# A two-layer trunk on one core: the attention's softmax steps in a fixed order of TensorE, and an operand tile 80 bytes further down

## The chip, the cores and the metric

The kernel runs on one core of a Trainium2 chip. The metric is the device time of one execution in microseconds (us). TensorE (PE) multiplies matrices; PEld is its loading of weights, which overlaps the multiplication. VectorE (DVE), ScalarE (ACT) and GpSimd (POOL) work element by element, SyncE (SP) issues the DMAs. Results of TensorE land in eight PSUM banks of 128 x 512 floats; everything else lies in SBUF. The three runs of the kernel before took 1333.64 us in the median (1331.63 to 1338.09).

## The reference

A trunk of two layers on 512 tokens of width 1024. Each layer is a mixer and then a SwiGLU feed-forward net, each inside a norm, a modulation by a conditioning vector (`c` times `ada_w`), and a second norm with a gate. The first mixer is a hybrid of pooling and a recurrence; the second, with which the change deals, is dilated attention:

```python
DIL_GROUPS = ((128, 1), (512, 4), (2048, 16))     # window, dilation
...
s = jnp.einsum('brnqhe,brnkhe->brnhqk', qs, kk) + bias
s = jnp.where(mask[None, None, :, None], s, -jnp.inf)
m = jnp.max(s, axis=-1, keepdims=True)
p = jnp.exp(s - m)
l = jnp.sum(p, axis=-1, keepdims=True)
...
w = l_all * jnp.exp(m_all - jnp.max(m_all, axis=0, keepdims=True))
o = jnp.sum(w * o_all, axis=0) / jnp.sum(w, axis=0)
...
return dilated_attention_mixer(h @ att_w_qkv[j], rel_bias) @ att_w_out[j]
...
def swiglu(h, w_in, w_out):
    a, b = jnp.split(h @ w_in, 2, axis=-1)
    return (jax.nn.silu(a) * b) @ w_out
```

There are 3 groups of 8 heads of 64 columns. The last step weights the groups by their sums, so the eight outputs of 64 columns are each one softmax over the keys of three groups.

## The kernel before, in words

Every large product is made of three matmuls in a rounded format: a value is split into a high part and a rest, and high by high, high by rest and rest by high are added in a PSUM bank. `split_into` splits operands, `split_next` the weights: ScalarE copies the high part (L351), VectorE or GpSimd subtracts (L284). All these matmuls go through the helper `mm` (L263). The moved operands lie in tile `h` (the layer's input, high and rest, 2 x 8 x 512 columns) or in `o`, the weights in `r`, in the "swing" tiles that change their owner between stages, and, while `o` and `h` are not needed for operands, there too.

Tile `o` (L197) is made 48 floats longer than its four units of 512 floats, and the slice that is used starts `O_OFF` floats in. By the program's addresses in a partition, `r`, `h` (behind its own offset) and the swing tiles begin at byte 128 of a block of 256; `o` begins at byte 64, that is 192 bytes past the others. The operands that move out of `o` are those of `out_project` when it is called without `late` (`operand`, `rr.get(n // HT, "o")`), for the first mixer's and for both feed-forward output products.

The attention layer runs in `attention` (from L1220). `project_head` makes the queries and keys of pair 0 of heads. Then `values(g, tiles)` makes, for each group g, the values in four PSUM banks: four blocks of 24 matmuls with 512 columns, in each of which one weight matrix is used up; after each block `ada_step` puts two products for the modulation of later stages (L403, 128 x 1025 elements) into VectorE's program, each with its own DMA. A pair of heads takes four steps r = 0 to 3 (quarter of the queries). In each the scores of both heads of three groups are made (28 short matmuls, L1329), VectorE adds the bias and takes the maximum (L1359), ScalarE takes the exponential and the sum (L1364), VectorE the reciprocal (L1366) and the product with it (L1367), TensorE transposes (L1370, eight of 128 x 128), and ScalarE copies the transposed weights out (L1372). `weighted` multiplies these with the values. Queries and keys of pairs 1 to 3 are six blocks of 24 matmuls a pair (`project`), copied from PSUM by `keep_qk` (L1236 on ScalarE, L1238 on VectorE). The output product with `w_ao` is `out_project` with `late`: 24 matmuls of 256 columns for each of four inputs, the first token half first, around the two halves of the weighted sum of pair 3.

The program is written stage by stage: all values, then pair by pair its queries and keys, its four steps, its weighted sum. A planner turns this order into one instruction list for each engine, by its own estimates of when an operand is there; a list is then executed in its order. `hold(...)` forbids it this for the engines named: they take the order of the program until `release()`. Before, the attention layer's first hold comes in `out_project`, after the third input of `w_ao`; up to there TensorE's order is the planner's, except that the two heads' scores alternate by added dependencies. Biases are loaded by SP (`load_biases`, six DMAs a pair, L1257), into tiles that the planner's order makes free.

Of the kernel before, what the change touches and what calls it, by code (L numbers as in the profile page):

```python
# [13 lines left out]
F32R = mybir.dt.float32r  # L14
# [4 lines left out]
P = 128  # L19
# [16 lines left out]
W0 = 259  # L36
# [7 lines left out]
O_OFF, H_OFF = 48, 8  # L44
# [136 lines left out]
def trunk(ctx: ExitStack, tc: tile.TileContext, a: dict, out: bass.AP, last: int = 3):  # L181
# [15 lines left out]
    rr.add("o", sb.tile([P, O_UNITS * UNIT + O_OFF], F32R, tag="o", name="o")[:, O_OFF:], O_UNITS)  # L197
# [558 lines left out]
    def out_project(s, base, n, srcs, ada_until, late=None):  # L756
# [3 lines left out]

        sets = [late[0], None] if late else [[bk.get() for _ in range(4)] for _ in range(2)]
# [414 lines left out]
    chain = out_project(0, w_ho, 8, mix_r, 20, (out_banks, EARLY, end_of_mixer, none, none))  # L1176
# [43 lines left out]
    def attention(s, chain):  # L1220
# [42 lines left out]
        def values(g, tiles):  # L1263
            vb = {c: bk.get() for c in tiles}
            for kk in range(4):
                hi, lo = weights(w_av + 4 * g + kk)
                for k in (2 * kk, 2 * kk + 1):
                    wh, wl = hi[:, (k % 2) * T : (k % 2 + 1) * T], lo[:, (k % 2) * T : (k % 2 + 1) * T]
                    for c in tiles:
# [10 lines left out]
            for c in tiles:  # L1280
                act.activation(VV[g][:, c, :], bk[vb[c]], AF.Copy)
                bk.free(vb[c])

        for g in range(3):
            values(g, (0, 1, 2, 3))

        o_rs = []
        for pair in range(4):
            qk_rs = []
            pt_rs = [ar.get(4) for _ in range(2)]  # L1290
            for x in (pair, pair + 1):
                if x < 4 and x not in biases_of:
                    load_biases(x)
            bias_r, bias_t = biases_of[pair]
            for i in range(6):
                if pair * 6 + i < N_QK:
                    qk_rs.append(head_rs[i])
                    continue
# [6 lines left out]
                qk_rs.append(r)  # L1305
            if pair == 3:
                ahead.update(load=14, split=4, f=2, r=0)
                out_banks = [bk.get() for _ in range(4)]
                rr.add("h", h_t, 2 * ND)
                rr.used["h"] = [k % ND < 4 for k in range(2 * ND)]  # L1310
                for _ in range(2):
                    split_next(0, pool)
                for i, r in enumerate(o_rs):
                    split_into(h_hi[:, i, :], h_lo[:, i, :], ar.ap(r))
                    ar.free(r)
            q0, k0, q1, k1, q2, k2 = (ar.ap(r) for r in qk_rs)
            PT = [ar.ap(r).rearrange("p (r s q) -> p r s q", r=4, s=4) for r in pt_rs]
            halves_of = [slice(64 * hh, 64 * hh + 64) for hh in range(2)]
            by_place = lambda z: z.rearrange("p (r i) -> p r i", r=4)
            two = lambda z: z.rearrange("p (s n) -> p s n", s=2)  # L1320
            for r in range(4):

                banks2 = [bk.get() for _ in range(2)]
                heads2 = list(enumerate(halves_of))[::-1]
                before = [None]

                def score(o, q, k, **kw):

                    i = pe.matmul(o, q, k, start=True, stop=True, skip_group_check=True, **kw).ins  # L1329
                    if before[0]:  # L1330
                        tc.add_manual_dep(i, before[0], NOSYNC, reason="two heads at a time")
                    before[0] = i.name

                qv = q0.rearrange("p (r j i) -> p r j i", r=4, j=4)
                for j in range(4):
                    js = slice(32 * j, 32 * j + 32)
                    for n in range(2 if j == 0 else 1):
                        for hh, ps in heads2:
                            kw = dict(tile_position=(64 * hh, 32 * j))
                            o = bk[banks2[hh]]  # L1340
                            if j == 0 and n == 0:
                                score(o[js, 0:P], far[ps, :], one_row[ps, :], **kw)
                            elif j == 0:
                                score(o[js, P : 2 * P], qv[ps, r, j, :], k0[ps, 0:P], **kw)
                            else:
                                score(o[js, 0 : 2 * P], qv[ps, r, j, :], k0[ps, (j - 1) * P : (j + 1) * P], **kw)
                for i, (q, k) in enumerate(((q1, k1), (q2, k2))):
                    for hh, ps in heads2:
                        qc, kc = (by_place(z)[ps, r, :] for z in (q, k))
                        o = bk[banks2[hh]][:, (2 + i) * P : (3 + i) * P]  # L1350
                        score(o, qc, kc)
                for hh in range(2):
                    b = banks2[hh]
                    sc_r = tr.get(1)
                    sc = tr.ap(sc_r)
                    base = bias_t[:, hh, 255 + r : 256 + r]
                    bias = bass.AP(base.tensor, base.offset, [list(base.ap[0]), [W0 - r, 2], [-1, 256]])
                    m = col(1)
                    dve.tensor_tensor_reduce(  # L1359
                        out=two(sc), in0=two(bk[b]), in1=bias, scale=-1.0, scalar=3e38, op0=ALU.add, op1=ALU.min, accum_out=m  # L1360
                    )
                    bk.free(b)
                    l = col(1)
                    act.activation(sc, sc, AF.Exp, bias=m, scale=-1.0, accum_out=l)  # L1364
                    rl = col(1)
                    dve.reciprocal(rl, l)  # L1366
                    dve.tensor_scalar(sc, sc, rl, None, ALU.mult)  # L1367
                    b = bk.get()
                    for i, seg in enumerate((1, 0, 2, 3)):
                        pe.transpose(bk[b][:, seg * P : (seg + 1) * P], sc[:, i * P : (i + 1) * P], ident)  # L1370
                    tr.free(sc_r)
                    act.activation(PT[hh][:, r, :, :], bk[b].rearrange("p (s q) -> p s q", s=4), AF.Copy)  # L1372
                    bk.free(b)
            for r in qk_rs:
                ar.free(r)
            ar.free(bias_r)

            def weighted(b, first, end):

                todo = []  # L1380
                for kb in range(4):
                    js = [j for j in (kb, kb + 1) if first <= j < end]
                    if js:
                        todo.append((0, kb, js))
# [162 lines left out]
```

## Time and profile before

| | |
|---|---|
| median of three runs | 1333.64 us (1331.63 to 1338.09) |
| profiled execution, time | 1336.7 us |
| profiled execution, span | 1334.9 us |
| TensorE busy | 1265.7 us, 95% |
| PEld / VectorE / ScalarE / GpSimd busy | 84% / 49% / 34% / 20% |
| granted clock of TensorE, mean | 0.97 |
| DMA | 164.25 MB, 123 GB/s in the mean |

A row of a group of instructions gives its line, the engine, the operation, what it writes and reads, how many there are, the busy time and the mean duration of one, and the engine's idle time just before them. Matmuls overlap: a duration in such a row (281 ns) is longer than the distance between two starts. Rows of the timeline give the start, the length, and in brackets the idle time before it and what ended it. In a row of a stretch the granted clock is a share of full speed.

### The profile page before, as it was taken

The page shows a single profiled execution, that of the slowest core. Times are in us where ns is not written, and L with a number is a line of the kernel's source. Part 1 is how long each engine was busy: PE and PEld are TensorE (multiplying, and loading weights), DVE is VectorE, ACT ScalarE, POOL GpSimd, SP SyncE. Part 2 cuts the span into 40 slices and gives each one's busy share as a digit, 9 for nine tenths or more (in the row PEclk, how much of TensorE's full clock was granted, in tenths as well). Part 3 has the DMA queues.
Part 4 walks back from the last instruction along what each step waited for, and adds up shares of the span by engine and source line. Part 5 has one row for each costly group of instructions (what it writes and reads, how often), then busy time and mean ns, then how long its engine had stood idle before and what let it go on. Part 6 is the DMA issues. An engine that isn't in the chain of part 4 may idle for free.

```text
span 1334.9 us, 20663 instructions
## 1 busy us (share of the span) xinstructions
PE 1265.7 (95%) x8672; PEld 1117.5 (84%) x8672; DVE 654.2 (49%) x965; ACT 455.3 (34%) x743; POOL 270.3 (20%) x141
## 2 busy tenths in 40 slices
PE   8897798999999999999999989987999999999997
PEld 6675588998888889999999768776898888889997
DVE  6997975855444223428576233343855222213415
ACT  4241434642222222317333333344552222222313
POOL 3541531411111111212211002030411111121002
PEclk9997899999999999999999899987999999999999
DMA  7855353225554222322277103150226222222301
GB/s 259 321 170 184 103 175 127 84 91 192 197 197 140 79 80 95 127 80 80 96 262 243 48 15 128 38 199 33 88 87 237 79 82 86 69 93 90 104 1 64
DMA packets 50383, 164.25 MB, mean 123 GB/s; under 512 B 5809, under 2 KB 11081, under 8 KB 50290
## 3 DMA queue, kind: packets, MB, share of 16 engines
q1 hardware_dynamic: 50290, 162.93, 35.9%
q8 instruction: 68, 1.11, 0.3%
q14 instruction: 25, 0.20, 0.0%
HBM read 160.78 MB, written 2.13 MB: 122 GB/s over the span
## 4 chain that ended last, share of the span: by engine, by line
PE 80%; DVE 13%; ACT 3%; issue 2%; DMA 2%; POOL 1%; SPq 0%; DVEq 0%; ACTq 0%; POOLq 0%
PE bank L263 76%; DVE ada_w L403 3%; PE bank L1370 1%; PE bank L1329 1%; DVE swing L937 1%; DVE t L1359 1%; DVE r L284 1%; DVE swing L938 1%; DVE swing L284 1%; DVE t L642 1%; ACT t L1364 0%; DVE h L681 0%; DVE f L646 0%; DVE h L539 0%; DMA f<-w_ho 0%
## 5 line engine op out<-in xcount | busy, mean ns | idle before, releaser
L263 PE MATMUL bank<-h,r 128*128 128x512 f32 (+1 forms) x2104 | 470.1, 365 | 15.7 <-DVE f L927 7.9
L263 PEld LDWEIGHTS bank<-h,r 128*128 128x128 f32 x2104 | 367.0, 193 | 79.6 <-ACT h L522 8.7
L263 PE MATMUL bank<-h,swing 128*128 128x512 f32 (+1 forms) x1664 | 325.0, 343 | 3.5 <-ACT swing L351 2.2
L263 PEld LDWEIGHTS bank<-h,swing 128*128 128x128 f32 x1664 | 268.1, 191 | 39.9 <-ACT swing L351 2.4
L284 POOL TENSOR_TENSOR r<-f,r 128x1024 fp32r<-128x1024 f32 x39 | 98.9, 2537 | 430.4 <-PE bank L263 301.1
L263 PE MATMUL bank<-o,swing 128*128 128x256 f32 x1280 | 159.2, 281 | 0.0
L263 PEld LDWEIGHTS bank<-o,swing 128*128 128x128 f32 x1280 | 154.2, 189 | 0.1
L351 ACT ACTIVATE r<-f 128x1024 fp32r<-128x1024 f32 x104 | 109.0, 1057 | 132.1 <-PE bank L263 93.3
L403 DVE SCALAR_TENSOR_TENSOR ada_w<-ada_w,sil 128x1025 f32<-128x1025 f32 x96 | 146.3, 1538 | 15.2 <-DMA ada_w<-ada 14.9
L284 DVE TENSOR_TENSOR r<-f,r 128x1024 fp32r<-128x1024 f32 (+1 forms) x51 | 73.8, 1448 | 161.3 <-PE bank L263 64.0
L284 DVE TENSOR_TENSOR swing<-f,swing 128x1024 fp32r<-128x1024 f32 x45 | 60.0, 1337 | 121.2 <-PE bank L263 81.6
L284 POOL TENSOR_TENSOR swing<-f,swing 128x1024 fp32r<-128x1024 f32 x27 | 66.3, 2456 | 259.3 <-PE bank L263 219.2
L351 ACT ACTIVATE swing<-f 128x1024 fp32r<-128x1024 f32 x80 | 83.5, 1057 | 85.7 <-PE bank L263 42.2
L263 PE MATMUL bank<-o,r 128*128 128x256 f32 x832 | 105.4, 281 | 0.0
L263 PEld LDWEIGHTS bank<-o,r 128*128 128x128 f32 x832 | 101.3, 189 | 0.1
L1193 ACT ACTIVATE t<-bank 128x512 f32<-128x512 f32 (+1 forms) x52 | 27.2, 531 | 175.3 <-PE bank L263 175.3
L263 PE MATMUL bank<-h,o 128*128 128x512 f32 (+1 forms) x312 | 81.6, 347 | 2.5 <-DVE h L681 1.7
L263 PE MATMUL bank<-r,h 128*128 128x512 f32 x288 | 70.9, 395 | 0.0
L263 PEld LDWEIGHTS bank<-r,h 128*128 128x128 f32 x288 | 61.8, 249 | 6.1 <-issue 0.4
L475 POOL TENSOR_TENSOR cst<-cst 128x2 f32<-128x2 f32 (+1 forms) x19 | 17.8, 937 | 232.7 <-DVE cst L473 232.7
L263 PEld LDWEIGHTS bank<-h,o 128*128 128x128 f32 x312 | 56.0, 192 | 10.6 <-DVE h L681 2.1
L284 DVE TENSOR_TENSOR o<-f,o 128x256 fp32r<-128x256 f32 (+2 forms) x37 | 24.5, 678 | 77.3 <-ACT o L565 74.2
(181 smaller groups left out, 1074.4 us busy)
## 6 DMA issues: line engine op xcount, KB each, us to landing
ada_w<-ada SPq DMA_DIRECT2D x96, 512.5 KB, 5.1
f<-w_fi SPq DMA_DIRECT2D x88, 512.0 KB, 4.6
f<-w_fo SPq DMA_DIRECT2D x44, 512.0 KB, 3.4
f<-w_aqk SPq DMA_DIRECT2D x24, 512.0 KB, 3.8
f<-w_av SPq DMA_DIRECT2D x12, 512.0 KB, 6.0
f<-w_qf SPq DMA_DIRECT2D x8, 512.0 KB, 5.2
f<-w_ho SPq DMA_DIRECT2D x8, 512.0 KB, 4.0
f<-x SPq DMA_DIRECT2D x8, 256.0 KB, 3.5
```

The costliest lines, as they stand in the source:

```text
L263: i = pe.matmul(o, lhsT, rhs, start=start, stop=stop, skip_group_check=True)
L284: eng.tensor_tensor(o, x, y, ALU.subtract)
L351: act.activation(hi, w, AF.Copy)
L403: dve.scalar_tensor_tensor(w, w, 1.0, sil, ALU.mult, ALU.mult, accum_out=mods[:, s, 2 * j + k : 2 * j + k + 1])
L475: pool.tensor_tensor(r, v, mhalf[:, 0:cols], ALU.pow)
L642: dve.tensor_tensor(us[i], us[i], rows, ALU.mult)
L937: dve.tensor_tensor(qv, qv, t_first.unsqueeze(2).broadcast_to([P, n, L]), ALU.mult)
L938: dve.tensor_tensor(kv, kv, t_second.unsqueeze(2).broadcast_to([P, n, L]), ALU.mult)
L1193: act.activation(tr.ap(sa)[:, cols], a, AF.Silu)
L1329: i = pe.matmul(o, q, k, start=True, stop=True, skip_group_check=True, **kw).ins
L1359: dve.tensor_tensor_reduce(out=two(sc), in0=two(bk[b]), in1=bias, scale=-1.0, scalar=3e38, op0=ALU.add, op1=ALU.min, accum_out=m)
L1370: pe.transpose(bk[b][:, seg * P : (seg + 1) * P], sc[:, i * P : (i + 1) * P], ident)
```

## The change

Two things change.

**Order.** `values` becomes a generator that stops after each block of 24 matmuls, so does the new `queries_and_keys`, and `fillers` chains 3 x 4 blocks of values and 3 x 6 blocks of queries and keys; `fill_in(n)` runs the next n of them. The softmax step is cut into `scores` and `transposed`. From the first block on TensorE is held to the program's order, which is now written out: scores of steps 0 and 1, a block, transposes of step 0, scores of step 2, a block, and so on. In pair 3 no blocks are left, and its steps stand between the inputs of `w_ao` (`between`, a new sixth entry of `late`, called after each 24 matmuls). TensorE is released before the four engines are held as before. The biases of pair 0 are loaded ahead of the first block, those of pair p + 1 after the last scores of pair p. The tiles `PT` of the transposed weights are allocated once and laid out with the group ahead of the step; heads go 0, 1 instead of 1, 0; the added dependencies go.

**Place.** `O_OFF` goes from 48 to 28 floats. The tile keeps its size, so that nothing else moves; the slice begins 80 bytes lower, at byte 240 of a block of 256, that is 112 bytes past `r` and the swing tiles.

```diff
-O_OFF, H_OFF = 48, 8
+O_OFF, H_OFF = 28, 8
...
-    rr.add("o", sb.tile([P, O_UNITS * UNIT + O_OFF], F32R, tag="o", name="o")[:, O_OFF:], O_UNITS)
+    rr.add("o", sb.tile([P, O_UNITS * UNIT + 48], F32R, tag="o", name="o")[:, O_OFF : O_OFF + O_UNITS * UNIT], O_UNITS)
...
             work = rest(0)
-            for _ in range(late[1] * 3 * ND):
-                next(work)
+            for i in range(late[1]):
+                for _ in range(3 * ND):
+                    next(work)
+                late[5](i)
             late[2]()
             hold(pe, act, dve, pool)
...
+        def queries_and_keys(pair):
             for i in range(6):
...
                 b = bk.get()
                 project(w_qk2 + pair * 6 + i - N_QK, b)
                 ada_step(44)
                 r = ar.get(1)
                 keep_qk(i, r, bk[b])
                 bk.free(b)
-                qk_rs.append(r)
...
+                qk_of[pair].append(r)
+                yield
+
+        def fillers():
+            for g in range(3):
+                yield from values(g)
+            for pair in range(1, 4):
+                yield from queries_and_keys(pair)
+
+        fill = fillers()
+
+        def fill_in(n=1):
+            for _ in range(n):
+                next(fill)
+
...
+        def transposed(r):
+            for hh in range(2):
+                sc_r = weights_of.pop((r, hh))
+                sc = tr.ap(sc_r)
+                b = bk.get()
+                for i, seg in enumerate((1, 0, 2, 3)):
+                    pe.transpose(bk[b][:, seg * P : (seg + 1) * P], sc[:, i * P : (i + 1) * P], ident)
+                tr.free(sc_r)
+                act.activation(PT[hh][:, :, r, :], bk[b].rearrange("p (s q) -> p s q", s=4), AF.Copy)
+                bk.free(b)
...
+        load_biases(0)
+        hold(pe)
+        fill_in()
+        for pair in range(3):
+            scores(pair, 0)
+            scores(pair, 1)
             for r in range(4):
...
+                fill_in()
+                transposed(r)
+                if r < 2:
+                    scores(pair, r + 2)
+            fill_in(8 if pair == 0 else 1)
+            output(pair)
+            fill_in(5 if pair == 0 else 1)
+        ahead.update(load=14, split=4, f=2, r=0)
+        scores(3, 0)
+        scores(3, 1)
+        out_banks = [bk.get() for _ in range(4)]
...
+        def between(i):
+            transposed(i)
+            if i < 2:
+                scores(3, i + 2)
+            else:
+                transposed(3)
+
         def first_half():
             late_b[0] = bk.get()
-            weighted(late_b[0], 0, 2)
+            weighted(3, late_b[0], 0, 2)
             split_late(0)
+            release()
```

TensorE's list where the first transposes of pair 0 stand, before (`far` and `swing` are read by scores, `cst,t` by transposes):

```order
L1329 MATMUL bank_77<-swing_0_5352 32x256
L1329 MATMUL bank_74<-swing_0_5352 32x256
L1329 MATMUL bank_77<-swing_0_5352 128x128
L1329 MATMUL bank_74<-swing_0_5352 128x128
L1329 MATMUL bank_77<-swing_1_5353 128x128
L1329 MATMUL bank_74<-swing_1_5353 128x128
L1370 MATMUL bank_70<-cst,t 128x128 x4
```

and now (rows `r,h` are a block of the values):

```order
L1343 MATMUL bank_73<-swing_1_5353 128x128
L1343 MATMUL bank_70<-swing_1_5353 128x128
L263 MATMUL bank_74<-r,h 128x512 x3
L263 MATMUL bank_77<-r,h 128x512 x3
L263 MATMUL bank_76<-r,h 128x512 x3
L263 MATMUL bank_75<-r,h 128x512 x3
L263 MATMUL bank_74<-r,h 128x512 x3
L263 MATMUL bank_77<-r,h 128x512 x3
L263 MATMUL bank_76<-r,h 128x512 x3
L263 MATMUL bank_75<-r,h 128x512 x3
L1374 MATMUL bank_72<-cst,t 128x128 x4
L1374 MATMUL bank_71<-cst,t 128x128 x4
```

The scores of the second step were followed at once by transposes; now 24 matmuls of the values stand between them, and values that stood ahead of all scores stand behind.

VectorE's list, where the first softmax steps of pair 0 stand (`ISA` is the sum with the bias and its maximum; RECIPROCAL and TENSOR_SCALAR belong to the softmax, L403 to the modulation), before:

```order
L403 SCALAR_TENSOR_TENSOR ada_w,cst<-ada_w,sil 128x1025
L284 TENSOR_TENSOR r<-f,r 128x1024
L1359 ISA t,cst<-bank_71,f 128x512
L1359 ISA cst 128x1
L1359 ISA t,cst<-bank_72,f 128x512
L1359 ISA cst 128x1
L1366 RECIPROCAL cst<-cst 128x1
L1367 TENSOR_SCALAR t<-t,cst 128x512
L1359 ISA t,cst<-bank_77,f 128x512
```

and now:

```order
L1351 ISA t,cst<-bank_70,f 128x512
L1351 ISA cst 128x1
L1358 RECIPROCAL cst<-cst 128x1
L403 SCALAR_TENSOR_TENSOR ada_w,cst<-ada_w,sil 128x1025
L1359 TENSOR_SCALAR t<-t,cst 128x512 x2
L403 SCALAR_TENSOR_TENSOR ada_w,cst<-ada_w,sil 128x1025
L1358 RECIPROCAL cst<-cst 128x1 x2
L1359 TENSOR_SCALAR t<-t,cst 128x512 x2
L284 TENSOR_TENSOR r<-f,o 128x1024
```

All products of the modulation stood ahead of the softmax; now they stand between its instructions.

TensorE's list at the steps of pair 3 (`h` rows are the output product), before:

```order
L1329 MATMUL bank_70<-swing_2_5361 128x128
L1329 MATMUL bank_71<-swing_2_5361 128x128
L263 MATMUL bank_76<-h,r 128x256 x6
L263 MATMUL bank_75<-h,r 128x256 x6
L263 MATMUL bank_72<-h,r 128x256 x6
L1370 MATMUL bank_74<-cst,t 128x128 x4
L1370 MATMUL bank_73<-cst,t 128x128 x4
L1329 MATMUL bank_73<-far 32x128
```

and now:

```order
L1343 MATMUL bank_75<-f 128x128
L1343 MATMUL bank_73<-f 128x128
L263 MATMUL bank_70<-h 128x256 x6
L263 MATMUL bank_74<-h 128x256 x6
L263 MATMUL bank_77<-h 128x256 x6
L263 MATMUL bank_72<-h 128x256 x6
L1374 MATMUL bank_71<-cst,t 128x128 x4
L1374 MATMUL bank_76<-cst,t 128x128 x4
L1334 MATMUL bank_75<-far 32x128
```

Before, the inputs of `w_ao` were used up between the first two steps; now one input stands ahead of each of the transposes of steps 0, 1 and 2, with none ahead of those of step 3 but the transposes of step 2.

More of the change, by code (lines that the diff above doesn't have):

```diff
@@ L1261, in attention, with values @@
         VV = [ar.ap(r).rearrange("p (c f) -> p c f", c=4) for r in v_rs]
-        def values(g, tiles):
-            vb = {c: bk.get() for c in tiles}
+        pt_rs = [ar.get(4, "sz") for _ in range(2)]
+        PT = [ar.ap(r).rearrange("p (s r q) -> p s r q", s=4, r=4) for r in pt_rs]
+        halves_of = [slice(64 * hh, 64 * hh + 64) for hh in range(2)]
+        qk_of = {0: head_rs, 1: [], 2: [], 3: []}
+        by_place = lambda z: z.rearrange("p (r i) -> p r i", r=4)
+        two = lambda z: z.rearrange("p (s n) -> p s n", s=2)
+        weights_of = {}
+        def values(g):
+            vb = [bk.get() for _ in range(4)]
             for kk in range(4):
@@ L1268, in values @@
                     wh, wl = hi[:, (k % 2) * T : (k % 2 + 1) * T], lo[:, (k % 2) * T : (k % 2 + 1) * T]
-                    for c in tiles:
+                    for c in range(4):
                         if g == 0:
@@ L1279, in values @@
                 ada_step(44)
[L1280 to L1294, printed above, removed]
+                if kk == 3:
+                    for c in range(4):
+                        act.activation(VV[g][:, c, :], bk[vb[c]], AF.Copy)
+                        bk.free(vb[c])
+                yield
+        def queries_and_keys(pair):
             for i in range(6):
-                if pair * 6 + i < N_QK:
-                    qk_rs.append(head_rs[i])
-                    continue
                 b = bk.get()
@@ L1304, in attention @@
                 bk.free(b)
-                qk_rs.append(r)
[L1306 to L1320, printed above, removed]
-            for r in range(4):
[L1323 to L1373, printed above, removed]
@@ L1403, in attention @@
-            if pair < 3:
-                b = bk.get()
-                weighted(b, 0, 4)
-                for r in pt_rs:
-                    ar.free(r)
-                r = ar.get(1, "f")
-                act.activation(ar.ap(r), bk[b], AF.Copy)
-                bk.free(b)
-                o_rs.append(r)
+                qk_of[pair].append(r)
+                yield
+        def fillers():
[3 more added lines that the diff above has]
+                yield from queries_and_keys(pair)
@@ new lines, in attention, with output @@
+        o_rs = []
+        def output(pair):
+            b = bk.get()
+            weighted(pair, b, 0, 4)
+            r = ar.get(1, "f")
+            act.activation(ar.ap(r), bk[b], AF.Copy)
+            bk.free(b)
+            o_rs.append(r)
+        load_biases(0)
[4 more added lines that the diff above has]
+            scores(pair, 1)
+            for r in range(4):
+                fill_in()
[5 more added lines that the diff above has]
+            fill_in(5 if pair == 0 else 1)
@@ L1413, in attention @@
+        ahead.update(load=14, split=4, f=2, r=0)
+        scores(3, 0)
+        scores(3, 1)
+        out_banks = [bk.get() for _ in range(4)]
+        rr.add("h", h_t, 2 * ND)
+        rr.used["h"] = [k % ND < 4 for k in range(2 * ND)]
+        for _ in range(2):
+            split_next(0, pool)
+        for i, r in enumerate(o_rs):
+            split_into(h_hi[:, i, :], h_lo[:, i, :], ar.ap(r))
+            ar.free(r)
         late_b = [None]
@@ L1434, in end_of_mixer @@
             ahead.update(load=14, split=14, f=2, r=4)
-        chain = out_project(s, w_ao, 4, (), 44, (out_banks, 3, first_half, second_half, end_of_mixer))
+        chain = out_project(s, w_ao, 4, (), 44, (out_banks, 3, first_half, second_half, end_of_mixer, between))
         rr.used["h"] = [False] * 2 * ND
```

96 lines of the change are left out of this document (69 added, 27 removed).

## The prediction

> **What bounds the kernel now.** I read the page first, then the stretches of the attention layer, then what its softmax steps wait for.
>
> ```profile
> span 1334.9 us, 20663 instructions
> PE 1265.7 (95%) x8672; PEld 1117.5 (84%) x8672; DVE 654.2 (49%) x965; ACT 455.3 (34%) x743; POOL 270.3 (20%) x141
> PEclk9997899999999999999999899987999999999999
> PE 80%; DVE 13%; ACT 3%; issue 2%; DMA 2%; POOL 1%; SPq 0%; DVEq 0%; ACTq 0%; POOLq 0%
> ```
>
> TensorE is busy for 95% of the span and carries 80% of the chain of waits. So time can come only from its idle holes, from a lowered clock, or from shorter matmuls. In the clock row the digits 23, 27 and 28 dip (the 4th and 5th too, in the first layer); with 33.4 us a digit these lie at 734–768 and 868–934 us, in the attention layer. Here is that layer, cut where the softmax begins and ends (columns: stretch; its length; busy time and count on PE, PEld, DVE, ACT, POOL; granted clock; DMA share; GB/s):
>
> ```profile
> 666.87:731.37 64.50, 64.50 (x278) 60.89 (x276) 45.85 (x65) 21.06 (x30) 10.54 (x4) 1.00 0.79 261
> 731.37:743.60 12.23, 9.47 (x101) 6.68 (x100) 6.81 (x19) 8.36 (x18) 0.00 (x0) 0.69 0.01 2
> 743.60:785.23 41.63, 41.63 (x238) 33.22 (x237) 7.99 (x18) 9.27 (x17) 2.39 (x1) 0.97 0.13 39
> 785.23:801.01 15.78, 11.32 (x141) 8.22 (x141) 10.04 (x33) 9.41 (x23) 0.00 (x0) 0.89 0.15 31
> 801.01:838.76 37.75, 37.75 (x200) 30.15 (x201) 11.24 (x8) 11.46 (x14) 7.22 (x3) 1.00 0.33 113
> 838.76:850.40 11.64, 8.62 (x125) 6.13 (x124) 6.28 (x20) 5.52 (x13) 0.00 (x0) 0.85 0.00 1
> 850.40:888.89 38.49, 38.49 (x210) 31.30 (x208) 13.54 (x23) 16.92 (x28) 4.83 (x3) 1.00 0.44 151
> 888.89:927.92 39.03, 26.71 (x258) 22.14 (x257) 15.00 (x37) 12.06 (x26) 6.14 (x2) 0.74 0.25 82
> sum 261.05, PE 238.50 PEld 198.74 DVE 116.74 ACT 94.05 POOL 31.12; mean PE 29.81 PEld 24.84 DVE 14.59 ACT 11.76 POOL 3.89
> ```
>
> The long stretches (values, then queries and keys) are full at clock 0.97 to 1.00; the four softmax stretches are idle for 2.76, 4.46, 3.02 and 12.32 us, and their clock is 0.69 to 0.89. The waits between 640 and 930 us (total, times, longest) name the partner:
>
> ```profile
> PE bank L1370 <- DVE t L1367: 17.4, 9, 3.0
> DVE ada_w L403 <- DMA ada_w<-ada: 10.8, 11, 2.2
> ```
>
> L1370 transposes the softmax weights, L1367 divides them by their sum: TensorE has no other work queued while VectorE and ScalarE do a softmax step.
>
> **The change, part 1: TensorE's order.** No arithmetic goes. What is to be had is the time that the layer takes above its work at full rate. For that, rows of TensorE alone (length, busy and count, clock, DMA share, GB/s; a count takes in the neighbours at the edges):
>
> ```profile
> 877.91:888.89 10.98, 10.98 (x49) 1.00 0.36 124
> 794.08:795.33 1.25, 1.25 (x29) 1.00 0.00 0
> 759.43:760.22 0.79, 0.79 (x10) 1.00 0.26 75
> 765.48:768.89 3.41, 3.41 (x50) 1.00 0.29 119
> 901.33:903.80 2.47, 2.47 (x23) 1.00 0.03 7
> ```
>
> They are two query or key blocks of 24 matmuls (5.49 each), one score step of two heads, its 8 transposes, the weighted sum of a pair, and 20 matmuls of the layer's output product (0.1235 each). The work at that rate: values 64.50; 18 blocks by 5.49 = 98.8; 16 steps by 1.25 + 0.79 = 32.6; three weighted sums 10.2 and half of one, 1.8 (an estimate, half of 3.41 rounded up); 72 output matmuls 8.9. Together 216.8, so 261.05 − 216.8 = 44.2 us are lost. Going by the stretches instead (length less busy time by clock, all but the first) gives 5.7 + 1.2 + 5.7 + 0 + 4.3 + 0 + 19.3 = 36 us. The count is the better of the two, because its terms are start to start and a busy row's end is modelled; the other is kept as a bound.
>
> Afterwards each step's scores stand at least one block ahead of its transposes. What must fit below a block is this chain (rows of VectorE; the pair of heads whose scores end at 894.28):
>
> ```profile
> 889.43 3.38 DVE L284 TENSOR_TENSOR r<-f,r 128x1024 fp32r<-128x1024 f32 x1
> 892.74 0.68 DVE L1238 COPY swing<-bank 128x512 f32<-128x512 f32 x1
> 894.30 0.69 DVE L1359 CUSTOM_DVE_ANT_1 t<-bank,swing 128x512 f32<-128x512 f32 x1 [0.88 <-PE bank L1329]
> 896.79 0.49 DVE L1367 TENSOR_SCALAR t<-t,cst 128x512 f32<-128x512 f32 x1
> ```
>
> From 894.30 to 897.28 it is 3.0 us for both heads, against 5.49 + 1.25 = 6.7 us from the first scores of a pair to their transposes, and over 12 us for later ones, so most steps vanish below the blocks. What stays:
>
> - Pair 0, first step. VectorE's queue now has products L403 of the modulation between this softmax's instructions, which wait for their weights:
>
> ```profile
> 675.28 1.23 DVE L403 SCALAR_TENSOR_TENSOR ada_w<-ada_w,sil 128x1025 f32<-128x1025 f32 x1 [1.31 <-DMA ada_w<-ada]
> ```
>
> 3.0 for the chain, three of these at 1.23, the other head pair's two maxima (1.3), and a wait of 0 to 2.2: 8.0 to 10.2 against 6.7, so TensorE waits 1.3 to 3.5; with a clock that falls, I take 3.5.
> - Starts of pairs 1 and 2: the last key block is copied out (0.68) before the last scores, which 1.1 us of other scores cover in part: 1 in all.
> - Pair 3. The same copy stands behind a weight split (3.38, then 0.68) and now with the splits of `h`; TensorE waited 2.33 there, and still does:
>
> ```profile
> 893.48 0.80 PE L1329 MATMUL bank<-swing 64*128 64x128 f32 x4 [2.33 <-DVE swing L1238]
> 921.62 1.97 PE L1370 MATMUL bank<-cst,t 128*128 128x128 f32 x8 [2.46 <-DVE t L1367]
> 924.28 3.16 PE L263 MATMUL bank<-swing,swing 128*64 128x256 f32 x40 [0.69 <-ACT swing L1372]
> ```
>
> Blocks are shorter here (24 by 0.1235 = 3.0 us), so the first and last transposes are covered by 4.2 and 3.8 us for a chain of 3.0: about 1 us late each, behind `h` splits. With the copies ahead of the weighted sum (0.69) and a lowered clock (2 by estimate) pair 3 keeps 3 + 2 + 0.7 + 2 = 7.7.
> - Banks: a new values group takes four banks while ScalarE copies out the last one: 1.5, an estimate from two copies of about 0.6.
>
> That is 13.7 us left of 36 to 44, a gain of 22 to 30; I take 29, nearer the count. All hidden is 42, the most. The six bias loads of pair 0 move ahead of two value weights on SP's queue, and pair 1's among the modulation loads; the value weights are loaded five ahead (some 28 us of TensorE), which hides the few us of issue, and nothing if the DMA were full (it is at 0.79). The new layout of the transposed weights and the order of heads change no count and no size: nothing, within a tenth of a copy.
>
> The Trainium skill ("TensorE: Matmul & The Clock Gate", section "Why this matters for your kernels") asks for no idle gap above about 3 us between bursts, so shorter ones should not cost the clock. By it, the small waits left would cost only themselves, and pair 3 would keep 5.7; the trace disagrees, since the first softmax stretch has 2.76 us of gaps in all and yet a clock of 0.69.
>
> **Part 2: the place of the operands.** By the program's addresses tiles `r`, swing and `h` begin at the same byte of each 256; `o` began 64 bytes before them (192 past), and now 112 past. Matmuls that move `o`:
>
> ```profile
> L263 PE MATMUL bank<-o,swing 128*128 128x256 f32 x1280 | 159.2, 281 | 0.0
> L263 PE MATMUL bank<-o,r 128*128 128x256 f32 x832 | 105.4, 281 | 0.0
> 503.90 22.78 PE L263 MATMUL bank<-o,swing 128*128 128x256 f32 x192
> 526.51 17.59 PE L263 MATMUL bank<-o,r 128*128 128x256 f32 x148
> 279.38 8.92 PE L263 MATMUL bank<-h,swing 128*128 128x256 f32 x73
> 288.14 0.40 PE L263 MATMUL bank<-h,r 128*128 128x256 f32 x2
> 262.48 0.28 PE L263 MATMUL bank<-h,o 128*128 128x256 f32 x1
> 268.92 0.28 PE L263 MATMUL bank<-h,o 128*128 128x256 f32 x1
> 1060.38 21.92 PE L263 MATMUL bank<-h,swing 128*128 128x512 f32 x96
> 1082.13 16.94 PE L263 MATMUL bank<-h,r 128*128 128x512 f32 x74
> ```
>
> Start to start: `o` against swing, 192 bytes, 22.61 us by 192 = 117.8 ns; `h` against swing, 0 bytes, 8.76 by 73 = 120.0; `h` against `o`, 64 bytes: six groups of one such and eight `h,r` last 6.44, so 1073 − 8 × 120.0 = 113. No row has 112 bytes. On the line between 64 (113) and 192 (117.8) it is 114.8: 3.0 ns by 2112 = −6.3 us, and +0.4 for 144 `h,o` matmuls that leave 64 bytes; I take −6. Below, a matmul costs no less than its columns: 512 take 21.75 by 96 = 226.6 ns, so 256 columns cost 226.6 − 120.0 = 106.6, and the least is −11.2 by 2112 = −24. Above stands the 0-byte row: +2.2 by 2112 = +5.
>
> The Trainium skill speaks against any effect ("SBUF — State Buffer", section "A bandwidth-pool intuition that's wrong": weight loads have a read port of their own). The three rows differ by 7 ns, which it does not explain; by it the sum would be 1305.
>
> The sum: 1336.7 (the profiled run; span 1334.9) − 29 − 6 = 1301.7. The median of the runs is 3.1 below the profiled run, so 1298.6: about **1299**.
>
> **Rivals.**
> - *The steps stay late by one us each.* VectorE and ScalarE also split weights, and their queues are in order. 1 us in each of the 14 steps that I cost at nothing and a clock of 0.97 (as in 743–785) over 217 us: +14 + 6.5, so 1319. For it: modulation products and splits stand between softmax instructions. Against it: 12 us of cover.
> - *The place is worth nothing, or costs:* 1299 + 6 = 1305, to 1310 with the 0-byte price. For it: the line is drawn through three points of different tiles.
> - *The gain comes back later:* the weights of the feed-forward layer come no sooner, and TensorE waits there for what it gained: 1299 + 29 = 1328, or 1334 if the second part goes too. Against it: the DMA share is 0.13 to 0.44 once values are done.
> - *Slower: a fixed order that cannot step aside.* TensorE may no longer take other work when a step is late, so if VectorE's queue is held by modulation loads and weight splits, each of 16 steps stalls and the clock stays low all along. At 0.89 (785–801) the work takes 216.8/0.89 = 243.6; with 2 us a step 275.6, which is 15 more than 261: 1334 + 15 − 6 = 1343. It decides from (261 + 6 − 243.6)/16 = 1.5 us a step. For it: waits of 2.0 to 3.0 us stand in the trace now. Against it: loads are late only in the values stage (10.8 us in all).
>
> **How the numbers follow.** My forecast 0.50, place worth nothing or less 0.24, steps late 0.12, given back 0.07, slower 0.07. The first three are faster by over 0.5% (6.7 us, about what a measurement of this kernel can tell): 0.86; given back is the same, 0.07; slower 0.07. The range goes from the forecast less the deeper gain of both parts (13 us by the count's limit, or 18 by the columns' limit; 16 taken) to the late steps: 1283 to 1320; it leaves out the last two cases and a little at the low end. The likeliest case alone has 1285 to 1312.
>
> **What would show it.** The page: TensorE's share near 97%, no dips of the clock between the values and the output product except at pair 3. The wait of transposes for L1359's scale (L1367 before) falls from 17.4 to below 5 us; layer length about 232. The o-rows start 115 ns apart against 117.8. I am wrong in part 1 if waits of over 1 us stand before most transposes or the feed-forward layer gains idle time; in part 2 if the o-rows are at 117.8 or above.

## The result, and the profile after

The changed kernel takes 1296.91 us in the median of four runs (1293.51 to 1298.13), against 1334.87 for the kernel before on the same chip: a ratio of 0.9712, 95% interval 0.968 to 0.9743, so 34 to 43 us less. Forecast were 1299 and 35 us less. Of the kernels below, one run of the kernel without cover in pairs 0 to 2 took 1888 us at a granted clock of 0.61 and is left out of its times.

The page of the profiled execution, lines that answer to those of before:

```profile
span 1291.7 us, 20674 instructions
PE 1236.8 (96%) x8672; PEld 1093.5 (85%) x8672; DVE 646.6 (50%) x965; ACT 453.5 (35%) x743; POOL 271.3 (21%) x141
PEclk9998899999999999999999999999999999999999
PE 81%; DVE 12%; ACT 3%; issue 2%; POOL 1%; DMA 1%; SPq 0%; DVEq 0%; ACTq 0%; POOLq 0%
```

The three dips of the clock in the second half of the row (digits 23, 27, 28) are gone; those of the first layer are still there. To see where the time went, both programs are cut at five places that they share: the first matmul that moves `o`, the last of the first feed-forward layer, the first output matmul behind pair 3's weighted sum, and the first and last `o` matmuls of the second feed-forward layer. The columns are the stretch, its length, busy time of PE and its count, then the other engines, the granted clock, DMA share and GB/s. Before:

```profile
498.24:625.60 127.36, 126.98 (x1073) 126.30 (x1072) 54.88 (x69) 44.87 (x76) 25.83 (x13) 1.00 0.29 96
625.60:927.92 302.32, 278.29 (x1860) 237.45 (x1858) 141.40 (x258) 111.77 (x196) 41.67 (x18) 0.94 0.36 119
927.92:1196.38 268.46, 264.36 (x1445) 228.41 (x1446) 103.64 (x143) 90.33 (x135) 50.20 (x25) 1.00 0.30 100
1196.38:1322.34 125.96, 125.96 (x1072) 125.96 (x1071) 41.65 (x51) 34.10 (x54) 13.33 (x7) 1.00 0.19 62
```

and after:

```profile
492.99:616.28 123.29, 122.53 (x1072) 121.89 (x1071) 55.13 (x69) 44.77 (x75) 26.16 (x13) 1.00 0.30 99
616.28:889.19 272.91, 264.74 (x1859) 228.77 (x1857) 133.25 (x258) 109.90 (x197) 40.99 (x18) 0.99 0.38 129
889.19:1157.64 268.45, 264.42 (x1444) 228.52 (x1445) 103.58 (x143) 90.35 (x135) 50.23 (x25) 1.00 0.30 103
1157.64:1279.14 121.50, 121.50 (x1073) 121.49 (x1072) 41.68 (x51) 34.16 (x54) 13.43 (x7) 1.00 0.20 63
```

The attention stretch lost 29.4 us: its idle time fell from 302.32 − 278.29 = 24.0 to 8.2, which is 15.9, and its busy time fell by 13.5 with the same matmuls, at a clock of 0.99 for 0.94 (busy time by clock is the same within the rounding of the clock: 278.29 × 0.94 = 261.6, 264.74 × 0.99 = 262.1). The two stretches of `o` matmuls lost 4.1 and 4.5. They hold all 2112 of these, 1056 each: in the trace only the two feed-forward output products move `o`, and the first mixer's does not. The feed-forward stretch between is the same to 0.01 us, so nothing was given back there. That makes 38.0, which is the difference of the medians. The spans differ by 5 us more, because the changed kernel's first stretch begins 5.2 us sooner (492.99 for 498.24). That is no effect of the change: with the order alone (below) it begins at 491.77, with the place alone at 495.23, and in the five other profiled runs whose tiles lie as in the changed kernel at 492.19 to 498.31.

TensorE's timeline after, around the steps, and two rows of VectorE:

```profile
660.65 4.42 PE L263 MATMUL bank<-o,h 128*128 128x512 f32 x18 [1.90 <-DVE swing L1241]
667.50 5.76 PE L263 MATMUL bank<-r,h 128*128 128x512 f32 x24
673.10 1.04 PE L1374 MATMUL bank<-cst,t 128*128 128x128 f32 x8
774.45 0.49 PE L1343 MATMUL bank<-swing 64*128 64x128 f32 x4 [0.81 <-DVE swing L1241]
867.20 0.49 PE L1343 MATMUL bank<-f 64*128 64x128 f32 x4 [0.77 <-issue]
871.07 2.89 PE L263 MATMUL bank<-h 128*128 128x256 f32 x22 [1.70 <-POOL h L284]
886.43 2.29 PE L263 MATMUL bank<-swing,swing 128*64 128x256 f32 x40 [0.35 <-ACT swing L1376]
...
667.58 1.41 DVE L403 SCALAR_TENSOR_TENSOR ada_w<-ada_w,sil 128x1025 f32<-128x1025 f32 x1
671.41 0.87 DVE L1359 TENSOR_SCALAR t<-t,cst 128x512 f32<-128x512 f32 x2
```

The first transposes of pair 0 (673.10) follow the block without a wait: VectorE had scaled their input by 672.28, 0.8 us ahead. No transposes of the attention layer wait for the scale any more, in none of the four pairs, where they had waited 17.4 us.

### The profile page after: what moved, and what is told of

Same layout as the page of the kernel before. It is cut to its first block, busy times and chain, and to the rows that moved or that the text cites. A ratio compares the mean times of both kernels' runs of the same rounds, so it can differ in the third digit from the quotient of the medians.

```text
span 1291.7 us, 20674 instructions
## 1 busy us (share of the span) xinstructions
PE 1236.8 (96%) x8672; PEld 1093.5 (85%) x8672; DVE 646.6 (50%) x965; ACT 453.5 (35%) x743; POOL 271.3 (21%) x141
## 4 chain that ended last, share of the span: by engine, by line
PE 81%; DVE 12%; ACT 3%; issue 2%; POOL 1%; DMA 1%; SPq 0%; DVEq 0%; ACTq 0%; POOLq 0%
PE bank L263 78%; DVE ada_w L403 4%; PE bank L1374 1%; DVE t L642 1%; PE bank L1343 1%; DVE swing L941 1%; DVE swing L284 1%; DVE f L646 1%; DVE swing L940 1%; POOL cst L475 1%; DVE h L681 0%; DVE t L603 0%; DVE r L284 0%; POOL h L284 0%; DMA f<-x 0%
## 5 line engine op out<-in xcount | busy, mean ns | idle before, releaser
L284 POOL TENSOR_TENSOR r<-f,r 128x1024 fp32r<-128x1024 f32 x39 | 100.2, 2570 | 391.1 <-PE bank L263 289.0
L263 PE MATMUL bank<-o,swing 128*128 128x256 f32 x1280 | 153.7, 276 | 0.0
L403 DVE SCALAR_TENSOR_TENSOR ada_w<-ada_w,sil 128x1025 f32<-128x1025 f32 x96 | 143.7, 1513 | 11.8 <-DMA ada_w<-ada 11.7
L263 PEld LDWEIGHTS bank<-o,swing 128*128 128x128 f32 x1280 | 149.1, 188 | 0.1
L284 DVE TENSOR_TENSOR r<-f,r 128x1024 fp32r<-128x1024 f32 (+1 forms) x51 | 65.1, 1277 | 167.3 <-PE bank L263 110.5
L284 POOL TENSOR_TENSOR swing<-f,swing 128x1024 fp32r<-128x1024 f32 x27 | 66.5, 2462 | 255.7 <-PE bank L263 209.0
L284 DVE TENSOR_TENSOR swing<-f,swing 128x1024 fp32r<-128x1024 f32 x45 | 59.9, 1335 | 119.9 <-PE bank L263 80.9
L263 PE MATMUL bank<-o,r 128*128 128x256 f32 x832 | 101.7, 275 | 0.0
L263 PEld LDWEIGHTS bank<-o,r 128*128 128x128 f32 x832 | 97.8, 188 | 0.1
L284 DVE TENSOR_TENSOR o<-f,o 128x256 fp32r<-128x256 f32 (+2 forms) x37 | 24.8, 687 | 74.1 <-ACT o L565 70.3
```

The costliest lines, as they stand in the source:

```text
L263: i = pe.matmul(o, lhsT, rhs, start=start, stop=stop, skip_group_check=True)
L284: eng.tensor_tensor(o, x, y, ALU.subtract)
L403: dve.scalar_tensor_tensor(w, w, 1.0, sil, ALU.mult, ALU.mult, accum_out=mods[:, s, 2 * j + k : 2 * j + k + 1])
```

## The experiments

**The place alone.** The kernel before, with one number changed (the tile keeps its size, as in the change):

```diff
-O_OFF, H_OFF = 48, 8
+O_OFF, H_OFF = 28, 8
```

> The kernel before with operand tile o 112 bytes past the weights instead of 192, nothing else. My theory (the distance between the moved operand and the weights sets the interval of the 256-column matmuls): the o matmuls start 113 ns apart as in the changed kernel, against 118, so 2112 of them save 8.5 to 10 us and the time is about 1326. Rival (the place does nothing, the changed kernel's shorter intervals come with the new order): intervals of 118 and 1335.

1323.23 us against 1334.03, ratio 0.9929 (0.9902 to 0.9956). Its stretches of `o` matmuls, and the attention between:

```profile
495.23:618.79 123.56, 122.77 (x1072) 122.00 (x1071) 55.42 (x69) 44.67 (x75) 26.17 (x13) 1.00 0.30 99
618.79:919.42 300.63, 276.21 (x1859) 235.40 (x1858) 141.48 (x258) 111.81 (x197) 41.76 (x18) 0.95 0.36 120
1187.87:1309.36 121.49, 121.49 (x1073) 121.49 (x1072) 41.69 (x51) 34.15 (x54) 13.43 (x7) 1.00 0.20 64
```

The `o` stretches are 3.8 and 4.5 us shorter, as in the changed kernel, and the attention has its old length but for 1.7 us. The place works by itself and is worth 8.3 us in the trace, 6 to 13 in the time.

**The order alone.** The changed kernel with `O_OFF` back at 48.

> The changed kernel with o at 192 bytes as before, so the new order alone. My theory: 29 us faster than before, about 1305, with the o matmuls back at 118 ns. Rival (the two parts depend on each other, or the order is worth all 38 us): 1297.

1303.67 us, ratio 0.9775 (0.9751 to 0.9798): 27 to 33 us less than before.

```profile
491.77:619.11 127.34, 126.72 (x1072) 126.03 (x1071) 55.05 (x69) 44.87 (x76) 25.84 (x13) 1.00 0.29 96
619.11:892.96 273.85, 265.88 (x1860) 230.34 (x1858) 133.23 (x258) 109.94 (x196) 41.53 (x18) 0.99 0.39 129
```

The `o` stretch is as before, the attention as after, to 1 us. The two parts add up: 8.3 and 28.5, against 38.0 together.

**Without cover in pairs 0 to 2.** Cover is here what TensorE has to do between a step's scores and its transposes. The order stays written out, two steps stay in flight (the next step's scores are issued ahead of a step's transposes), but the four blocks of a pair stand ahead of its scores.

```diff
+            fill_in(4)
             scores(pair, 0)
             scores(pair, 1)
             for r in range(4):
-                fill_in()
                 transposed(r)
```

> The changed kernel with the four blocks of each of pairs 0 to 2 moved ahead of the pair's scores: the order stays written out, but no block stands between a step's scores and its transposes. My theory (the blocks cover the softmax steps): each pair loses about what pairs 1 and 2 lost before, 5 to 8 us with the clock, so 15 to 24 in all and 1312 to 1321, with waits of transposes for the scale of 1 to 3 us at most steps. Rival (fixing the order and the new layout did it, not the cover): 1297 to 1301.

1318.82 us in the median of three runs (1317.63 to 1322.97), ratio 0.9897 (0.9865 to 0.9929), within what was expected from the cover. The attention stretch, a part of it around pair 0, and TensorE's waits there:

```profile
621.16:918.65 297.49, 274.46 (x1859) 234.93 (x1857) 132.81 (x258) 111.18 (x197) 40.19 (x18) 0.96 0.36 121
690.00:712.00 22.00, 15.41 (x158) 0.84 0.38 126
...
699.08 1.97 PE L1374 MATMUL bank<-cst,t 128*128 128x128 f32 x8 [4.54 <-DVE t L1359]
709.09 0.66 PE L1374 MATMUL bank<-cst,t 128*128 128x128 f32 x4 [1.51 <-DVE t L1359]
```

24.6 us are back (272.91 to 297.49): 14.9 idle and 9.7 of longer busy time. So much is the cover worth where two steps are in flight. With pair 3 as changed, the stretch is only 4.8 us shorter than under the planner's order (302.32), and pair 3 alone gives more than that (below): a written order without the blocks is worse in pairs 0 to 2 than the planner's, which had put some of them between.

**Is the longer busy time the clock?** The same kernel, with 12 dummy matmuls ahead of each step's transposes in pairs 0 to 2:

```diff
             for r in range(4):
+                keep_warm(12, of=ident)
                 transposed(r)
```

> The kernel with the steps of pairs 0 to 2 uncovered, with 12 dummy matmuls (128 columns, 1.34 us at full rate, 12 steps: 16 us) ahead of each step's transposes, which keep TensorE busy while it would wait. Uncovered, the layer is 24.6 us longer than changed: 14.9 of it idle, 9.7 more of busy time. My theory (the 9.7 are the clock that idle time lowers): the dummies take the place of idle time and give the clock back; less the 9.7, plus some 5 of dummies that overshoot: about 1316, with granted clocks near 1 in the softmax stretches. Rival (the longer busy time isn't the clock): 1321 plus the 5, 1326.

1328.04 us, ratio 0.9955 (0.9934 to 0.9976), above both forecasts: the price of a dummy was wrong. Each `keep_warm(12)` shows as 24 matmuls in the trace and takes 2.8 us, not 1.34:

```profile
620.04:924.97 304.93, 296.21 (x2147) 261.25 (x2146) 132.34 (x258) 111.67 (x197) 40.42 (x18) 0.99 0.35 118
690.00:712.00 22.00, 19.73 (x235) 1.00 0.36 125
...
700.83 2.94 PE L263 MATMUL bank<-cst 128*128 128x128 f32 x24
703.62 1.04 PE L1374 MATMUL bank<-cst,t 128*128 128x128 f32 x8
```

Twelve times 2.79 (700.83 to 703.62) are 33.5 us of dummies. Idle time fell from 23.0 to 8.7. Had the rest kept its length, the stretch would be 297.5 − 14.3 + 33.5 = 316.7; it is 304.9, so the real work became 11.8 us shorter once TensorE did not stop, and the granted clock around pair 0 went from 0.84 to 1.00. So the 9.7 us of longer busy time were the clock. That the time rose is no evidence against it: more was put in than was given back.

**Without cover in pair 3.** All four steps ahead of the output product, two in flight.

```diff
         def between(i):
-            transposed(i)
-            if i < 2:
-                scores(3, i + 2)
-            else:
-                transposed(3)
+            pass
+
+        for i in range(3):
+            transposed(i)
+            if i < 2:
+                scores(3, i + 2)
+        transposed(3)
```

> The changed kernel with the four steps of pair 3 all ahead of the output product, pairs 0 to 2 as changed. The pair's stretch is 23.9 us in the changed kernel and 39.0 before. My theory (cover): the four steps in a row lose what a pair of the kernel without cover loses, 24.6/3 = 8 us, or more with the clock: 1305 to 1312. Rival (pair 3 gained because key copy and splits of h come sooner, not by cover): at most 1300.

1300.5 us (ratio to before 0.9747, 0.9719 to 0.9774), below the 1305 to 1312 expected and at the edge of the rival. The stretch of pair 3 (end of the last key block to the first output matmul behind the weighted sum), and its waits:

```profile
864.73:893.39 28.66, 22.90 (x257) 18.91 (x256) 15.51 (x36) 13.73 (x29) 7.04 (x3) 0.88 0.52 184
...
869.75 0.74 PE L1374 MATMUL bank<-cst,t 128*128 128x128 f32 x4 [2.35 <-DVE t L1359]
871.57 1.11 PE L1374 MATMUL bank<-cst,t 128*128 128x128 f32 x4 [1.08 <-DVE t L1359]
```

In the changed kernel it is

```profile
865.30:889.19 23.89, 20.60 (x257) 17.65 (x256) 15.66 (x36) 13.04 (x28) 8.10 (x3) 1.00 0.57 193
```

and before it was 39.03. So of pair 3's gain of 15.1 us the cover gives only 4.8 (23.89 to 28.66). Something else gives 10.4.

**One step in flight in pair 3.** Before, the scores of a step stood behind the transposes of the one ahead (904.61, 908.39, 910.43, 914.23 in its timeline); now two steps' scores are issued ahead of any transposes. The kernel above, with

```diff
         scores(3, 0)
-        scores(3, 1)
...
         for i in range(3):
             transposed(i)
-            if i < 2:
-                scores(3, i + 2)
+            scores(3, i + 1)
         transposed(3)
```

> The kernel with pair 3 uncovered, and only one of its steps in flight: scores, transposes, scores, transposes, ahead of the output product. Pair 3's stretch is 39.0 us before, 28.7 uncovered and 23.9 changed; so 4.8 of its 15.1 us are cover. My theory now: the other 10.3 come from two steps in flight (the next step's scores stand ahead of a step's transposes, as they did not in pair 3 before); then this kernel has a stretch of about 37 to 39 and 1309 to 1311. Rival (they come from where the copies and splits of h stand): still about 29, 1301.

1313.03 us, ratio 0.9848 (0.9813 to 0.9883).

```profile
870.72:912.97 42.25, 26.45 (x258) 22.17 (x257) 14.61 (x36) 14.63 (x29) 7.03 (x3) 0.76 0.35 125
...
883.56 1.94 PE L1374 MATMUL bank<-cst,t 128*128 128x128 f32 x8 [3.87 <-DVE t L1359]
890.14 1.94 PE L1374 MATMUL bank<-cst,t 128*128 128x128 f32 x8 [2.44 <-DVE t L1359]
896.24 0.82 PE L1374 MATMUL bank<-cst,t 128*128 128x128 f32 x4 [2.45 <-DVE t L1359]
```

The stretch is 42.25, above the 37 to 39 expected and far from the rival's 29, so where the copies and splits of `h` stand is not what gave the gain. Every step waits 2.4 to 3.9 us for the whole chain, and the clock is 0.76, as it was 0.74 before. It is 3.2 longer than before, where some output matmuls stood between. The second step in flight is worth 13.6 us of pair 3 where there is no cover. Of the kernel before, which had some, it is the likely cause of the 10.4 us; no run takes those apart.

**One step in flight, with cover, in pairs 0 to 2.**

```diff
-            scores(pair, 0)
-            scores(pair, 1)
             for r in range(4):
+                scores(pair, r)
                 fill_in()
                 transposed(r)
-                if r < 2:
-                    scores(pair, r + 2)
```

> The changed kernel with one step in flight in pairs 0 to 2: scores of a step, a block, its transposes, then the next scores. Cover is 5.5 us a step, the chain of a step 3.0 to 4. My theory (a cover longer than the chain is enough): 1297 to 1302, with waits in pair 0 alone, where products of the modulation stand between. Rival (two in flight are needed beside the cover): over 1 us late at most of the 12 steps, 1309 or more.

1299.18 us, ratio 0.9744 (0.9713 to 0.9775), with an overlap with the changed kernel's.

```profile
618.22:894.66 276.44, 267.25 (x1859) 230.23 (x1857) 131.81 (x258) 110.65 (x197) 41.63 (x18) 0.99 0.39 130
```

The layer is 3.5 us longer than in the changed kernel and idle for 9.2 instead of 8.2. Where a block is longer than the chain, the second step is worth little. The reverse does not hold: two steps in flight without blocks lost 24.6 us in these pairs.

**Other distances.** First `h` as well at 112 bytes past the weights (`h_t` made 64 floats longer, so that later tiles keep their places in each 256 bytes):

```diff
-O_OFF, H_OFF = 28, 8
+O_OFF, H_OFF = 28, 36
...
-    h_t = sb.tile([P, H_OFF + 2 * ND * T], F32R, tag="h", name="h")[:, H_OFF:]
+    h_t = sb.tile([P, 72 + 2 * ND * T], F32R, tag="h", name="h")[:, H_OFF : H_OFF + 2 * ND * T]
```

> The changed kernel with tile h also 112 bytes past the weights, instead of 0 (h and o then lie 0 apart). If the distance rules for every moved operand: some 1500 matmuls of 256 columns go from 120 to 113 ns and some 2700 of 512 columns from 227 to about 220, so 10 to 29 us less: 1268 to 1287. Rival (something of tile o alone, or the long matmuls hide it): no change for the 512-column ones, 1287 to 1297.

1302.13 us, ratio to before 0.9754 (0.9722 to 0.9786): not the gain that was expected, and above the rival's 1287 to 1297 too. The interval overlaps that of the changed kernel, and the first `o` matmul came 7.2 us later (500.21 for 492.99), so a loss in the time is not shown. 113 matmuls of 256 columns and 96 of 512 that move `h`, in the changed kernel:

```profile
239.40 13.80 PE L263 MATMUL bank<-h,swing 128*128 128x256 f32 x113
1021.64 21.92 PE L263 MATMUL bank<-h,swing 128*128 128x512 f32 x96
```

and here:

```profile
242.57 13.11 PE L263 MATMUL bank<-h,swing 128*128 128x256 f32 x113
1027.64 22.35 PE L263 MATMUL bank<-h,swing 128*128 128x512 f32 x96
```

The short ones gain 6 ns each, as `o` did; the long ones lose 4.5 ns, where a gain of 7 was expected, and there are more of them. At this place the 256 columns gain and the 512 do not.

Three more kernels with other numbers of `O_OFF` and `H_OFF` in the same lines (32, 16; 20, 4; 12, 24), and a fourth (26, 52), one profiled run each:

> The changed kernel with o 128 bytes past the weights and h 32 (h is 160 past o); read from the intervals. So far, 256 columns: 0 bytes 120 ns, 64 114, 112 113, 144 and 192 118; 512 columns: 0 227, 64 230, 112 231, 144 233. Theory A (a shape over the distance with one low place near 64 to 112): o at 128 between 113 and 118, h at 32 between 114 and 120 for 256 and 227 to 230 for 512 columns. Rival B (what counts is the distance in blocks of 128 bytes, so that 128 is like 0): o at 120.

> The changed kernel with o 80 bytes past the weights and h 240 (16 before them; h is 160 past o). Theory A (one low place near 64 to 112): o at 113 or a little less; h at 240 between 118 and 120 for 256 columns, 227 to 233 for 512. If o at 80 is below 113, a better place than that of the change exists; each ns is 2.1 us.

> The changed kernel with o 48 bytes past the weights, h 64. Intervals of 256 columns so far, o: 80 bytes 118, 112 113, 128 119, 192 118; h: 0 120, 32 117, 112 114, 240 117; of 512 columns, h: 0 227, 32 234, 112 231, 240 230 to 234. A line between neighbours has failed: 80 and 128 are both at 118. Theory C (48 bytes past a multiple of 64 is the good place, 112 being one): o at 48 is at 113. Rival D (no such period): 117 to 120. For h at 64 I have no rule: 113 to 120, and 227 to 234 for 512 columns.

> The changed kernel with o 104 bytes past the weights, h 176. Theory C (48 past a multiple of 64): h at 176 has 113 to 114 for 256 columns, as at 112; 231 for 512. o at 104, 8 bytes beside the good place: 113 if the place is some 16 bytes wide, 118 if it is exact. Rival D: h at 176 has 117 to 120.

The times were 1326, 1312, 1314 and 1318 us, all above the changed kernel. The row of 192 matmuls that move `o`, in the changed kernel (start to start 520.23 − 498.47 = 21.76, 113.3 ns each; a row's length is 0.16 us more):

```profile
498.47 21.92 PE L263 MATMUL bank<-o,swing 128*128 128x256 f32 x192
520.23 16.93 PE L263 MATMUL bank<-o,r 128*128 128x256 f32 x148
```

then with `o` at 128 bytes, at 80, at 48 and at 104:

```profile
514.69 22.94 PE L263 MATMUL bank<-o,swing 128*128 128x256 f32 x192
```

```profile
505.96 23.20 PE L263 MATMUL bank<-o,swing 128*128 128x256 f32 x192
```

```profile
509.23 22.88 PE L263 MATMUL bank<-o,swing 128*128 128x256 f32 x192
```

```profile
503.23 23.20 PE L263 MATMUL bank<-o,swing 128*128 128x256 f32 x192
```

Less 0.16, by 192, that is 118.6, 120.0, 118.3 and 120.0 ns. Of the places tried for `o`, 112 bytes alone is low: 8 bytes less cost 6.7 ns, 16 more 5.3. Theory A (one low place from 64 to 112) and theory C (48 past a multiple of 64) fall; B (128 like 0) is not shown either, 118.6 being neither 113 nor 120. D (no such period, 117 to 120) holds. No rule was found.

Is it the byte at which the moved operand begins, whatever the weights? The traces of two kernels that differ in `O_OFF` alone answer it, the changed kernel and the one with the order alone: their second layer has 24 matmuls that move `h`, which stayed in its place, against weights in `o`, which did not. In the changed kernel (`o` at 112) and with `o` back at 192:

```profile
844.13 5.83 PE L263 MATMUL bank<-h,o 128*128 128x512 f32 x24
```

```profile
846.49 5.75 PE L263 MATMUL bank<-h,o 128*128 128x512 f32 x24
```

They differ by 3 ns each (the first such group, at 776.13 and 778.68, by 4). So the place of the weights counts too. Nor is it the distance alone: at 64 bytes `h` against weights in `o` had 113 ns in the kernel before, and `h` moved to 64 past the swing tiles has 8.60 us by 73 = 117.8:

```profile
283.11 8.76 PE L263 MATMUL bank<-h,swing 128*128 128x256 f32 x73
291.71 0.40 PE L263 MATMUL bank<-h,r 128*128 128x256 f32 x2
```

Both places seem to matter together; how is open.

## Why the prediction was right, and where it was not

**The bound.** TensorE's idle time and its clock in the softmax stretches were what there was to take. The attention stretch lost 15.9 us of idle time and 13.5 of busy time. That the latter is the clock is shown by the granted clock (busy time by clock stayed the same) and, for the 9.7 us that came back without cover, by the dummies.

**Part 1, the sum.** 29 forecast, 28.5 measured with the order alone in the trace, 27 to 33 in the time. That it lay near the count minus the waits left (30) rather than the clock's sum (22) was right. ("All hidden is 42" does not follow from the count, which has 44.2.) The waits left, term by term:
- Pair 0's first step: 3.5 forecast, 0 measured. What failed is the count of products of the modulation in between: three and a wait for their weights were priced, and between the maxima and the scale at 671.41 there were two (667.58 and one more behind it), without a wait. The chain took 5.9 us (666.35 to 672.28) for the 8.0 to 10.2 forecast, less than the cover of 6.7.
- Starts of pairs 1 and 2: 1 forecast, 0.8 measured at pair 1, none at pair 2.
- Pair 3: 7.7 forecast; 0.8, 1.7 and 0.35 of waits up to the weighted sum, and the clock stayed at 1.00; the transposes, forecast a us late twice, did not wait. The wait of 1.7 is for GpSimd's split of the first output weights (L284), which was not in the list.
- Banks: 1.5 forecast where a group of values follows another; none there, but 1.9 at the very first block, which waits until VectorE copies out pair 0's queries and keys.
- Not priced: the seams, where TensorE goes from one kind of matmul to another. A block lasts 5.6 us between steps (667.50 to 673.10) against 5.49 in a run of two. The stretch keeps 272.91 − 41.27 (what lies ahead of the values: 666.87 − 625.60) − 216.8 = 14.8 us above its work at full rate, near the 13.7 forecast but made of other things: 8.2 idle at most, and for the rest seams are the likely cause, which no run took apart. That the two sums agree is in part luck: the waits listed here come to 5.6 us.

**Part 1, the reason.** "Most steps vanish below the blocks" holds for pairs 0 to 2: without blocks 24.6 us come back. For pair 3 it is a third of the truth. The prediction counted its lost time as one with that of the other pairs and did not see that its steps had gone one at a time. Cover gives 4.8 of its 15.1 us; the other 10.4 most likely come from the second step in flight, which is worth 13.6 where there is no cover (28.7 against 42.3).

**Part 2.** 6 forecast, 8.3 measured. The term that was mis-sized is the interval at 112 bytes, 114.8 by a line between 64 and 192; it is 113.3. The line itself is refuted: 104 and 128 bytes lie on it at 114.5 and 115.4 and have 120.0 and 118.6. That the forecast came near was chance. The bounds around it (106.6 to 120.0) held, and the side effect on the `h,o` matmuls was small. The Trainium skill's separate read port for weight loads ("SBUF — State Buffer", section "A bandwidth-pool intuition that's wrong") had been read as speaking against any effect; the place alone is faster by 0.4 to 1.0%. Whether the ports have to do with it no run here shows.

**The rivals.** *Steps late by one us*: no transposes wait at all. *The place is worth nothing*: refuted by the place alone. *Given back later*: the feed-forward stretch is 268.45 for 268.46. *Slower, by VectorE's queue*: the loads of the modulation are late at times, but not where TensorE waits; without the blocks, TensorE waits 4.54 us at pair 0's first step (699.08), with products of the modulation among its softmax instructions on VectorE.

## What to carry to other kernels

A chain through other engines can be taken off TensorE's path in two ways, by work between its halves and by issuing the next step's first half before this one's second; where there is no work to put between, the second is worth more than it looks (13.6 us of one pair). Blocks longer than the chain made it nearly needless (3.5 us of three pairs), while it did not replace the blocks (24.6 us). Reckon with the clock as well as the gaps: here 15.9 us of idle time took another 13.5 with them. When the place of an operand matters, scan it in the kernel itself, for each width of matmul and with the weights where they will lie, and trust no line between two places.

## What the runs showed of the hardware

- Repeated short waits lower the clock. Without cover, waits of 0.5 to 4.5 us around pair 0 came with 0.84, and dummies there gave 1.00; waits of 2.4 to 3.9 in pair 3 came with 0.76. A single wait of 1.7 us in the changed kernel's pair 3 left it at 1.00. The Trainium skill ("TensorE: Matmul & The Clock Gate", section "Why this matters for your kernels") warns of gaps above some 3 us; in pair 3 uncovered none is above 2.35 and the clock is 0.88.
- The start-to-start time of matmuls with 256 columns goes from 113.3 to 120.0 ns with the byte at which the moved operand begins, the weights in their place, and 8 bytes can make all of that (112 and 104). With the moved operand in its place, moving the weights changes it too: 24 matmuls of 512 columns took 5.75 and 5.83 us.
- The place that is best of those tried at 256 columns is not at 512: 96 of these take 22.35 us with `h` at 112 and 21.92 at 0.
- The first `o` matmul comes at 492.19 to 498.31 in the profiled runs with the tiles in the same places, a spread of some 6 us. It is there already at the row of 73 `h` matmuls some 219 us ahead of it (273.31 to 279.43). The stretches behind repeat to 0.3 us where the code is the same (268.46 and 268.45; 123.29 and 123.56).
